# Seven products of quarters for the down projection of a gated MLP in fp32, in place of eight

## The chip, the cores and the metric

One core of a Trainium2 chip runs the whole program in one launch. The metric is device microseconds from the first to the last instruction of that core, as the median of several runs. TensorE (PE) multiplies, its weight loads are listed apart (PEld); VectorE (DVE), ScalarE (ACT) and GpSimd (POOL) do the elementwise work; SyncE (SP) issues most DMAs.

## The reference

Two sequences of 512 tokens, each with 16 meta tokens in front (T = 528), go through two layers: a mixer (attention in layer 0, a gated linear recurrence, hgrn, in layer 1) and then the MLP that the change is about. All in fp32:

```python
def conv_ffn(h, w_up, conv_w, conv_b, w_down):
    u = h @ w_up                                   # 1024 -> 5632
    u = sum(up[:, j:j + L] * conv_w[j] for j in range(3)) + conv_b
    val, gate = jnp.split(u, 2, axis=-1)           # 2 x 2816 gated features
    return (jax.nn.silu(gate) * val) @ w_down      # 2816 -> 1024

h = layer_norm(ALPHA * h + conv_ffn(h, ...), ln_gain[layer, 1], ln_bias[layer, 1])
```

The output is both sequences without the meta tokens.

## The kernel before

**Numbers in two parts.** TensorE multiplies in a rounded fp32 (F32R). Each operand x is split into a high part (a rounding copy, on ScalarE) and a low part (x minus the high part, on VectorE or GpSimd, `split` at L397 for features, `Weights.split` at L104 for weights), and each product is three matmuls: high by high, high by low, low by high. So every tile that TensorE reads costs one copy and one subtraction.

**Weights.** `Weights` (L78) walks a plan, one entry for each piece of up to 1024 columns, in the order of use. `get` takes a piece and keeps two ahead: `_load` issues its DMA into one of three raw buffers, `_split` makes the two parts into one of three pairs of buffers. For the down projection the low parts go to VectorE and GpSimd in turn (L154).

**The up stage** (from L1496) makes one of 22 pairs of feature blocks (j) at a time for both sequences. It computes the product of the first 1024 by two blocks with seven products of quarters in place of eight, with sums of weights made on GpSimd (`_mix`, L162), then the convolution, silu and the gate, and stores the gated block to `g_dr` in DRAM.

**The down stage** (from L1650) multiplies 2816 gated features (22 tiles of 128, index k) with the weights, one sequence after the other (s), the 8 output tiles of 128 in three groups (`MG`: 3, 3 and 2). In layer 0 a tile's 528 tokens go as two matmuls of 264 columns, in layer 1, where the meta tokens are dropped, as one of 512. In the first group of a sequence `load_g` (L1532) fetches each tile of features into one of four staging buffers and splits it, low parts on VectorE and GpSimd in turn; they stay for the other groups. When a group is done, VectorE reads PSUM, adds the residual in the same operation (L1670) and sums up for LayerNorm.

**LayerNorm** runs beside the matmuls as side work: a generator whose next step is emitted at a `tick()` between matmuls. Sequence 0's stands under sequence 1's matmuls, layer 0's sequence 1 under the start of the next layer. In layer 1 the last two output tiles of sequence 1 are done in two halves of 256 tokens (`last_group`, L1541), so that only the second half's LayerNorm is left behind the last matmul.

**Order.** The queue of each engine is fixed when the kernel is built: of the instructions that the planner takes to be ready, the one that stands first in the program goes first. On the chip each engine then runs its queue in that order, and waits on semaphores. PSUM has four tiles of two banks (`mtile`).

Of the kernel before, what the change touches and what calls it, by code (L numbers as in the profile page):

```python
# [19 lines left out]
D = 1024  # L20
META = 16
T = 528
# [36 lines left out]
MG = ((0, 1, 2), (3, 4, 5), (6, 7))  # L59
# [5 lines left out]
def down_pieces(ms):  # L65

    per = 1024 // (128 * len(ms))
    return [range(k, min(k + per, NJ)) for k in range(0, NJ, per)]
# [10 lines left out]
class Weights:  # L79


    def __init__(self, tc, pool, plan):
# [6 lines left out]
        self.kept = self.last = None  # L89
# [28 lines left out]
    def _load(self):  # L118
# [3 lines left out]
        for ap in () if place in self.loaded else aps:  # L122
# [13 lines left out]
    def _split(self):  # L136
# [13 lines left out]
        if key[0] == "mix":  # L150
            self.ready.append(self._mix(key, raws))
        else:
            n = math.prod(aps[0].shape) // 128
            on_dve = key[0] in ("rope", "v", "rows") or key[0] == "up" and (key[2] == 0 or key[3] in (0, 1, NJ + 2)) or key[0] == "down" and (self.ns % 2 or key[1:4] in ((1, 1, 2), (1, 1, 3)))  # L154
            self.ready.append(self.split(raws[0][:, :n], n, self.nc.vector if on_dve else self.nc.gpsimd))
# [24 lines left out]

    def get(self, key):
        assert self.plan[self.pos][0] == key, (self.plan[self.pos][0], key)
        last = len(self.plan)
        while self.ns < min(self.pos + 2, last):
            while self.nd < min(self.ns + 2, last):
                self._load()
            self._split()
        while self.nd < min(self.ns + 2, last):
# [65 lines left out]
def weight_plan(a):  # L254
# [15 lines left out]
    def block(layer):  # L270
        def down(s, g, i):
            n = 128 * len(MG[i])
            for ks in down_pieces(MG[i]):
                add(("down", layer, s, g, ks[0]), a[f"w_dn{layer}_{i}"][:, ks[0] * n : (ks[-1] + 1) * n])
# [13 lines left out]
        for s in range(2):  # L288
            for g in range(len(MG)):
                down(s, g, g)  # L290
        if layer == 1:
            down(1, 3, 2)
# [25 lines left out]
def tile_trunk(ctx: ExitStack, tc: tile.TileContext, a: dict, dbg=None):  # L318
# [16 lines left out]

    kr_dr = dram.tile([2, 2, 128, T], F32, tag="kr", name="kr_dr")
# [991 lines left out]
    def mlp_block(layer, dest):  # L1328
# [131 lines left out]
        def gated():  # L1460
            return [dp.tile([128, 2, T], F32, tag=f"c{half}", name="c", bufs=2 - half) for half in range(2)]
# [29 lines left out]
        for j in range(NPL, NJ):  # L1491
# [12 lines left out]
            nc.scalar.copy(e5, p5)  # L1504
            w = W.get(("mix", layer, j, 2))
# [15 lines left out]
            nc.sync.dma_start(g_dr[layer][j][:, :, f0:], ca)  # L1521
        close(d_cm, mix_cm[1], mix_cm[0], act_cm[1])

        g2_cm, g2 = open_pool(f"g2{layer}", side="right")
        g1_cm, g1 = open_pool(f"g1{layer}", side="right")
        e_cm, ep = open_pool(f"e{layer}", bufs=3, side="left")
        out = x_dr[2:4]
        t0 = META if dest == "out" else 0
# [231 lines left out]
```

## Time and profile before

| | us |
|---|---|
| median of 3 runs | 2959.49 (2959.28 to 2959.75) |
| the profiled execution | 2960.56 |
| its span, first to last instruction | 2958.7 |
| TensorE busy | 2841.1 |
| VectorE, ScalarE, GpSimd busy | 2014.8, 1339.4, 1314.3 |

The profile is of one execution. "Busy" is the time in which an engine had an instruction under way. Matmuls are pipelined: one of 264 columns is listed with 0.28 us, but the next begins after 0.12 us, so the pace is read from counts in a window. A row of a group gives line, engine, operation, output and inputs, shape and count; a wait gives the engine and line that waited, and what it waited for.

### The profile page before, as it was taken

To read this page: it belongs to the slowest core of one execution; us is meant where nothing else is said; L and a number is where in the kernel's file an instruction comes from. 1 tells how busy PE (TensorE), PEld (TensorE's weight loads), DVE (VectorE), ACT (ScalarE), POOL (GpSimd) and SP (SyncE) were. 2 spreads that over 40 slices of the span, in tenths; PEclk is the share of its full clock that TensorE was granted. 3 is DMA by queue.
4 is the path that set the end of the run, shared out by engine and by line. 5 is a ranking of instruction groups with operands and counts; after the bars stand their busy time and mean duration, and the time that the engine had idled before them with its cause. 6 is when DMAs were issued, how large, how long until landed. Compare 5 with 4: busy or idle time off the path is not lost.

```text
span 2958.7 us, 54755 instructions
## 1 busy us (share of the span) xinstructions
PE 2841.1 (96%) x22402; PEld 2749.5 (93%) x22402; DVE 2014.8 (68%) x2680; ACT 1339.4 (45%) x2275; POOL 1314.3 (44%) x889
## 2 busy tenths in 40 slices
PE   8889999999899999999999999999998999999997
PEld 8888999899899999999999999999998999998886
DVE  5687788866988888535275565555669888885346
ACT  3355555543634344434265554444436444444343
POOL 5344444453576776434242220000315767765333
PEclk9999999999999999999999999999999999999999
DMA  7423322357512222654477564444775222226543
GB/s 254 158 89 114 100 87 80 98 204 276 183 65 85 82 71 90 193 157 146 148 251 249 206 207 169 144 150 144 240 259 210 72 87 73 79 84 195 168 145 118
DMA packets 144138, 438.51 MB, mean 148 GB/s; under 512 B 19744, under 2 KB 28960, under 8 KB 125200
## 3 DMA queue, kind: packets, MB, share of 16 engines
q1 hardware_dynamic: 139392, 425.39, 43.1%
q10 hardware_dynamic: 3168, 5.43, 0.6%
q8 instruction: 176, 2.88, 0.4%
q0 software_dynamic: 1328, 4.19, 0.4%
q14 instruction: 74, 0.61, 0.1%
HBM read 288.22 MB, written 142.34 MB: 146 GB/s over the span
## 4 chain that ended last, share of the span: by engine, by line
PE 41%; DVE 3%; ACT 2%; DMA 2%; issue 1%; POOL 1%; DVEq 0%; ACTq 0%; POOLq 0%; SPq 0%
PE mm L414 5%; PE mm L416 5%; PE mm L415 5%; PE mm L1483 4%; PE mm L1484 4%; PE mm L1485 4%; PE mm L1660 2%; PE mm L1659 2%; PE mm L1658 2%; PE mm L892 1%; PE mm L893 1%; PE mm L891 1%; PE a L1065 1%; PE a L1038 1%; PE mm L422 1%
## 5 line engine op out<-in xcount | busy, mean ns | idle before, releaser
L414 PE MATMUL mm<-ah,w 128*128 128x264 f32 (+1 forms) x2528 | 735.8, 291 | 22.1 <-ACT w L106 9.5
L415 PE MATMUL mm<-al,w 128*128 128x264 f32 (+1 forms) x2528 | 722.3, 286 | 7.9 <-DVE al L402 7.9
L416 PE MATMUL mm<-ah,w 128*128 128x264 f32 (+1 forms) x2528 | 723.5, 286 | 4.5 <-DVE w L107 2.3
L414 PEld LDWEIGHTS mm<-ah,w 128*128 128x128 f32 x2528 | 481.1, 190 | 29.2 <-ACT w L106 9.5
L415 PEld LDWEIGHTS mm<-al,w 128*128 128x128 f32 x2528 | 481.9, 191 | 10.1 <-DVE al L402 9.5
L416 PEld LDWEIGHTS mm<-ah,w 128*128 128x128 f32 x2528 | 481.3, 190 | 4.9 <-DVE w L107 2.5
L107 POOL TENSOR_TENSOR w<-wraw,w 128x1024 fp32r<-128x1024 f32 (+3 forms) x126 | 267.3, 2124 | 431.8 <-ACT w L106 400.6
L106 ACT CAST w<-wraw 128x1024 fp32r<-128x1024 f32 (+3 forms) x262 | 242.6, 928 | 342.9 <-PE mm L1660 223.0
L1483 PE MATMUL mm<-ah,w 128*128 128x264 f32 (+1 forms) x1216 | 345.9, 284 | 7.3 <-ACT w L106 7.3
L1485 PE MATMUL mm<-ah,w 128*128 128x264 f32 (+1 forms) x1216 | 345.8, 284 | 2.5 <-DVE w L107 2.5
L1484 PE MATMUL mm<-al,w 128*128 128x264 f32 (+1 forms) x1216 | 344.9, 284 | 0.0
L1659 PE MATMUL mm<-gl,w 128*128 128x264 f32 (+1 forms) x1012 | 322.6, 319 | 4.2 <-DVE gl L402 4.2
L1660 PE MATMUL mm<-gh,w 128*128 128x264 f32 (+1 forms) x1012 | 321.2, 317 | 3.8 <-DVE w L107 2.0
L1658 PE MATMUL mm<-gh,w 128*128 128x264 f32 (+1 forms) x1012 | 323.1, 319 | 0.9 <-DVE acc L1670 0.9
L107 DVE TENSOR_TENSOR w<-wraw,w 128x1024 fp32r<-128x1024 f32 (+2 forms) x136 | 158.0, 1163 | 220.5 <-ACT w L106 220.4
L1483 PE MATMUL mm<-th,w 128*128 128x264 f32 (+1 forms) x912 | 260.5, 286 | 8.3 <-ACT e L1497 8.3
L1485 PE MATMUL mm<-th,w 128*128 128x264 f32 (+1 forms) x912 | 260.1, 285 | 0.0
L1484 PE MATMUL mm<-tl,w 128*128 128x264 f32 (+1 forms) x912 | 259.9, 285 | 0.0
L1483 PEld LDWEIGHTS mm<-ah,w 128*128 128x128 f32 x1216 | 230.3, 189 | 7.8 <-ACT w L106 7.8
L1485 PEld LDWEIGHTS mm<-ah,w 128*128 128x128 f32 x1216 | 230.2, 189 | 2.9 <-DVE w L107 2.9
L1484 PEld LDWEIGHTS mm<-al,w 128*128 128x128 f32 x1216 | 230.3, 189 | 0.0
L1660 PEld LDWEIGHTS mm<-gh,w 128*128 128x128 f32 x1012 | 191.2, 189 | 17.9 <-DVE w L107 2.2
(335 smaller groups left out, 7195.9 us busy)
## 6 DMA issues: line engine op xcount, KB each, us to landing
kept_dr<-w SPq DMA_DIRECT2D x73, 1024.0 KB, 6.6
w<-kept_dr SPq DMA_DIRECT2D x73, 1024.0 KB, 5.4
wraw<-w_up SPq DMA_DIRECT2D x88, 512.0 KB, 4.1
wraw<-w_dn SPq DMA_DIRECT2D x88, 384.0 KB, 3.3
wraw<-w_hg SPq DMA_DIRECT2D x32, 512.0 KB, 4.4
wraw<-w_dn SPq DMA_DIRECT2D x25, 512.0 KB, 3.6
gr<-g_dr SPq DMA_DIRECT2D x44, 264.0 KB, 3.4
gr<-g_dr SPq DMA_DIRECT2D x44, 256.0 KB, 3.6
```

The costliest lines, as they stand in the source:

```text
L106: self.nc.scalar.copy(h[:, :n], src)
L107: engine.tensor_tensor(l[:, :n], src, h[:, :n].bitcast(F32), op=ALU.subtract)
L414: mm(out, wh[:, ws], xh[:, x0 + k, cs], start=first and i == 0, stop=False)
L415: mm(out, wh[:, ws], xl[:, x0 + k, cs], start=False, stop=False)
L416: mm(out, wl[:, ws], xh[:, x0 + k, cs], start=False, stop=last and i == n - 1)
L422: mm(ps[c][:, :w], ones, src[:, t0 + c * w : t0 + (c + 1) * w], start=True, stop=True)
L1483: mm(out, wh[:, ws], bh, start=k == 0, stop=False)
L1484: mm(out, wh[:, ws], bl, start=False, stop=False)
L1485: mm(out, wl[:, ws], bh, start=False, stop=k == 3)
L1658: mm(o, wh[:, ws], gh[:, cs], start=k == 0, stop=False)
L1659: mm(o, wh[:, ws], gl[:, cs], start=False, stop=False)
L1660: mm(o, wl[:, ws], gh[:, cs], start=False, stop=k == NJ - 1)
```

## The change

The weight matrix (2816 by 1024) and the gated features (2816 by both sequences' tokens) are each cut into quarters: features into even and odd tiles (11 each) and, for each sequence, into the first and second half of its tokens; output tiles into 0 to 3 and 4 to 7. The four quarters of the result then come from seven products in place of eight, in the order 1, 6, 5, 7, 3, 2, 4. Products 1, 3 and 2 take a quarter of the features as it is, products 1, 2 and 4 a quarter of the weights; the other operands are sums of quarters:

- Sums of features for 6 and 5 are made in the up stage by two subtractions on GpSimd for each pair of tiles (`pair_sums`) and stored to a new array `t_dr`; for 7 and 4 one more subtraction on GpSimd is made at loading (`load_f`).
- Sums of weights for 6, 5, 7 and 3 are made at loading (`_down`), from up to three blocks; one sum stays in SBUF (`W.slots`).
- A product has two groups of two output tiles; each takes 11 tiles of features for both sequences, six matmuls for one output tile and both sequences (in layer 1 three matmuls of 512 columns, two sequences of 256 side by side). Product 4 is done for one sequence at a time.
- Each product's features are loaded and split again (`load_f`), for the next product in the second group of the running one, into 12 buffers for 11 tiles; low parts on VectorE, each third one on GpSimd.
- Results go from PSUM into the quarters that take them (an addition on VectorE, product 1 a copy on ScalarE); residuals are added in a step of their own.
- LayerNorm runs for halves of each sequence (264 or 256 tokens): the second halves are final after product 3, the first halves after product 4.

```diff
+NP = NJ // 2
+DOWN = "1657324"
+FBUFS = 12
...
+    def _down(self, key, raws):
+        q, g, b = key[2], *key[4:]
+        n = down_columns(b)                      # 1024, 1024, 768
+        even, odd = (nc.vector, nc.gpsimd) if b % 2 == 0 else (nc.gpsimd, nc.vector)
+        src = raws[0][:, :n]
+        if q not in "124":
+            s2 = self.slots[g, b]
+            if q == "6":
+                odd.tensor_tensor(src, src, raws[1][:, :n], op=ALU.add)
+                nc.vector.tensor_tensor(s2, src, s2, op=ALU.subtract)
+                src = s2
+            else:
+                odd.tensor_tensor(src, src, s2, op=ALU.add if q == "5" else ALU.subtract)
+        return self.split(src, n, even)
...
+        def pair_sums(i):
+            x, y = done.pop(2 * i), done.pop(2 * i + 1)
+            nc.gpsimd.tensor_tensor(x[:, :, hs[1]], x[:, :, hs[1]], x[:, :, hs[0]], op=ALU.subtract)
+            nc.gpsimd.tensor_tensor(x[:, :, hs[0]], y[:, :, hs[1]], x[:, :, hs[1]], op=ALU.subtract)
+            nc.sync.dma_start(t_dr[layer][i][:, :, t0:], x[:, :, t0:])
...
+        def load_f(q, i):
+            e = nc.gpsimd if i % 3 == 2 else nc.vector
...
+            if q in "165":
+                r = raw({"1": g(0, 0), "6": t[:, :, hs[0]], "5": t[:, :, hs[1]]}[q])
+            else:
+                r = raw(g(1, q in "73"))
+                if q in "74":
+                    less = raw(g(0, 1) if q == "7" else t[:, :, hs[0]])
+                    nc.gpsimd.tensor_tensor(r, r, less, op=ALU.subtract)
+            h = fp.tile([128, 2, wd], F32R, tag="fh", name="fh", bufs=FBUFS)
+            l = fp.tile([128, 2, wd], F32R, tag="fl", name="fl", bufs=FBUFS)
+            split(h, l, r, nc.scalar, e)
...
+        def group(q, s, g, after):
+            for i in range(NP):
+                if i % 4 == 0:
+                    wh, wl = W.get(("dn", layer, q, s, g, i // 4))
+                if (q, i) not in fs:
+                    load_f(q, i)
...
+                if after and g == 1:
+                    load_f(after, i)
+                tick()
...
+        def add_squares(q, xs, first=False):
+            for k, x in enumerate(xs):
+                sq = q if first and k == 0 else small("sq")
+                nc.scalar.activation(sq, x, AF.Square)
+                if sq is not q:
+                    nc.gpsimd.tensor_tensor(q, q, sq, op=ALU.add)
+
+        def shift_half(s, c):
+            x = [acc[m][:, s, hs[c]] for m in range(NK)]
+            nc.gpsimd.tensor_tensor(s1, x[0], x[1], op=ALU.add)
+            for k in (2, 3):
+                tt(s1, s1, x[k], op=ALU.add)
...
+            for k in range(4):
+                tt(x[k], x[k], mu, op=ALU.subtract)
+            for m in range(4, NK):
+                if c:
+                    tt(x[m], x[m], mu, op=ALU.subtract)
+                else:
+                    y = xs[m][:, s]
+                    nc.vector.scalar_tensor_tensor(y, y, ALPHA, mu, op0=ALU.mult, op1=ALU.subtract)
+                    nc.gpsimd.tensor_tensor(x[m], x[m], y, op=ALU.add)
+            add_squares(q, x[:4], True)
+            if c:
+                nc.gpsimd.tensor_tensor(s1, x[4], x[5], op=ALU.add)
+                for k in (6, 7):
+                    tt(s1, s1, x[k], op=ALU.add)
+                add_squares(q, x[4:])
+                yield from finish_half(s, c, [(0, s1), (1, q)])
...
+        def last_tiles(s, g, pss):               # product 4: two tiles, first half of sequence s
+            for y, ps in zip(x, pss):
+                tt(y, y, ps, op=ALU.add)
+            if g == 0:
+                nc.gpsimd.tensor_tensor(s1, *x, op=ALU.add)
+                add_squares(q, x)
+                return
+            if s == layer:                       # squares and tiles summed by TensorE instead
...
+            else:
+                for y in x:
+                    tt(s1, s1, y, op=ALU.add)
+                add_squares(q, x)
+            later(finish_half(s, 0, parts), 1)
+
+        def finish_half(s, c, parts):
...
+            for k in range(NK):
+                (nc.vector if k in (1, 4, 6) else nc.gpsimd).tensor_tensor(y, y, mu, op=ALU.subtract)
+            newton(r, v, t)
+            for k in range(NK):
+                nc.vector.scalar_tensor_tensor(y, y, prm[:, base + k : base + k + 1], r, op0=ALU.mult, op1=ALU.mult)
+                nc.scalar.activation(y, y, AF.Identity, bias=prm[:, base + 8 + k : base + 9 + k])
...
+                elif s == 0:
+                    split(act[0][0][:, k, h], act[0][1][:, k, h], y, nc.scalar, nc.gpsimd if k % 2 else nc.vector)
...
+        for n, q in enumerate(DOWN[:-1]):
+            for g in range(2):
+                pss = group(q, 0, g, DOWN[n + 1])
...
+            if q == "3":
+                for s in range(2):
+                    later(shift_half(s, 1))
...
+        for s in range(2):
+            later(shift_half(s, 0))
+        for s in range(2):
+            for g in range(2):
+                pss = group("4", s, g, None)
...
+                last_tiles(s, g, pss)
```

## Rows read from the trace of the kernel before

**Rows 1.** The page: the span, and busy time of each engine.

```profile
span 2958.7 us, 54755 instructions
PE 2841.1 (96%) x22402; PEld 2749.5 (93%) x22402; DVE 2014.8 (68%) x2680; ACT 1339.4 (45%) x2275; POOL 1314.3 (44%) x889
```

**Rows 2.** Busy time and count of each engine in six stretches of both layers.

```profile
core 0: us, PE busy (x) PEld busy (x) DVE busy (x) ACT busy (x) POOL busy (x), PEclk, DMA share, GB/s
820.00:1190.00 370.00, 365.93 (x2997) 365.72 (x2996) 314.84 (x273) 151.33 (x200) 260.65 (x127) 1.00 0.24 80
1202.50:1463.00 260.50, 253.78 (x2070) 252.45 (x2069) 103.08 (x115) 93.82 (x132) 102.83 (x59) 1.00 0.51 157
1240.00:1260.00 20.00, 20.00 (x167) 20.00 (x166) 4.92 (x6) 3.62 (x5) 4.97 (x3) 1.00 0.53 161
2682.50:2903.00 220.50, 217.59 (x936) 176.26 (x935) 86.49 (x94) 84.02 (x117) 88.66 (x51) 0.99 0.54 169
2700.00:2720.00 20.00, 20.00 (x87) 16.17 (x86) 7.99 (x8) 9.93 (x15) 14.07 (x9) 1.00 0.87 283
2903.00:2941.50 38.50, 34.96 (x273) 34.41 (x272) 32.43 (x39) 16.65 (x27) 12.34 (x10) 0.96 0.37 115
```

**Rows 3.** TensorE's waits, 1195 to 1475: us in total, times, longest.

```profile
PE mm L1660 <- DVE w L107: 2.0, 1, 2.0
PE mm L1659 <- DVE gl L402: 2.0, 1, 2.0
PE mm L1660 <- POOL w L107: 1.7, 1, 1.7
```

**Rows 4.** TensorE's longest wait from 2675 to the end.

```profile
PE mm L1623 <- DVE w L107: 3.5, 1, 3.5
```

**Rows 5.** Instructions by line or tile: ns min/median/max, first and last start, shapes.

```profile
L107 DVE TENSOR_TENSOR w<-wraw,w x136: 669/1218/2607, 9.5 to 2934.7; 128x1024 fp32r<-128x1024 f32 x80, 128x768 fp32r<-128x768 f32 x48, 128x512 fp32r<-128x512 f32 x8
L107 POOL TENSOR_TENSOR w<-wraw,w x126: 723/2362/3012, 25.2 to 2892.0; 128x1024 fp32r<-128x1024 f32 x63, 128x768 fp32r<-128x768 f32 x52, 128x256 fp32r<-128x256 f32 x8, 128x512 fp32r<-128x512 f32 x3
L402 POOL TENSOR_TENSOR gl<-gr,gh x44: 1285/1340/2243, 1199.4 to 2813.3; 128x528 fp32r<-128x528 f32 x22, 128x512 fp32r<-128x512 f32 x22
L402 DVE TENSOR_TENSOR gl<-gr,gh x44: 678/1095/2330, 1197.6 to 2811.9; 128x528 fp32r<-128x528 f32 x22, 128x512 fp32r<-128x512 f32 x22
L1511 DVE TENSOR_TENSOR u<-u,mm x38: 679/693/706, 832.0 to 2682.0; 128x528 f32<-128x528 f32 x19, 128x516 f32<-128x516 f32 x19
```

**Rows 6.** Timeline of VectorE and GpSimd: start us, duration us, what.

```profile
1199.42 3.54 POOL L402 TENSOR_TENSOR gl<-gr,gh 128x528 fp32r<-128x528 f32 x2
1211.25 1.81 POOL L107 TENSOR_TENSOR w<-wraw,w 128x768 fp32r<-128x768 f32 x1 [0.99 <-ACT w L106]
...
1199.95 1.83 DVE L402 TENSOR_TENSOR gl<-gr,gh 128x528 fp32r<-128x528 f32 x1
1201.71 0.69 DVE L1511 TENSOR_TENSOR u<-u,mm 128x528 f32<-128x528 f32 x1
1208.12 0.94 DVE L107 TENSOR_TENSOR w<-wraw,w 128x768 fp32r<-128x768 f32 x1
1211.29 2.33 DVE L402 TENSOR_TENSOR gl<-gr,gh 128x528 fp32r<-128x528 f32 x1
```

**Rows 7.** Groups by shape: busy us, mean ns, then idle before and releaser.

```profile
L107 POOL TENSOR_TENSOR w<-wraw,w 128x768 fp32r<-128x768 f32 x52 | 100.3, 1930 | 156.6 <-ACT w L106 125.4 <-DMA wraw<-w_dn 19.9 <-issue 11.1
L107 POOL TENSOR_TENSOR w<-wraw,w 128x256 fp32r<-128x256 f32 x8 | 5.8, 730 | 5.5 <-ACT w L106 5.5
L1001 DVE TENSOR_TENSOR qo<-qd,cross 128x256 f32<-128x256 f32 x32 | 13.4, 417 | 0.0
L1596 POOL TENSOR_TENSOR acc<-acc,gr 128x256 f32<-128x256 f32 x10 | 8.4, 873 | 15.0 <-ACT gr L1588 15.0
L1596 DVE TENSOR_TENSOR acc<-acc,gr 128x256 f32<-128x256 f32 x6 | 5.1, 873 | 0.0
```

More of the change, by code (lines that the diff above doesn't have):

```diff
@@ L121, in _load @@
         place = piece_place(key)
-        for ap in () if place in self.loaded else aps:
+        for i, ap in enumerate(() if place in self.loaded else aps):
+            if key[0] == "dn" and i == 2:
+                r = self.slots[key[4], key[5]]
+                self.nc.sync.dma_start(r, ap)
+                raws.append(r)
+                continue
             r = self.pool.tile([128, 1024], F32, tag="wraw", name="wraw", bufs=3)
@@ L270, in block, with down @@
     def block(layer):
[L271 to L274, printed above, removed]
+        def down(q, s):
+            blocks = {"1": "11", "6": "212211", "5": "11", "7": "22", "3": "12", "2": "12", "4": "22"}[q]
+            for g in range(2):
+                for b in range(3):
+                    cs = slice(1024 * b, 1024 * b + down_columns(b))
+                    aps = [a["w_dn"][layer, int(blocks[i]) - 1, int(blocks[i + 1]) - 1, g][:, cs] for i in range(0, len(blocks), 2)]
+                    add(("dn", layer, q, s, g, b), *aps)
         for s in range(2):
@@ L287, in block @@
                 add(("mix", layer, j, i))
[L288 to L292, printed above, removed]
+        for q in DOWN:
+            for s in range(2 if q == "4" else 1):
+                down(q, s)
     for ks in FIRST_ROWS:
@@ L1460, in gated, with load_pair @@
         def gated():
-            return [dp.tile([128, 2, T], F32, tag=f"c{half}", name="c", bufs=2 - half) for half in range(2)]
+            return [dp.tile([128, 2, T], F32, tag=f"c{half}", name="c", bufs=3 - 2 * half) for half in range(2)]
+        t0 = META if dest == "out" else 0
+        wd = half_of(t0)
+        hs = [slice(t0 + c * wd, t0 + (c + 1) * wd) for c in range(2)]
+        done = {}
+        def load_pair(i):
+            for j in (2 * i, 2 * i + 1):
+                if j not in done:
+                    done[j] = dp.tile([128, 2, T], F32, tag=f"p{j % 2}", name="p", bufs=1)
+                    nc.sync.dma_start(done[j][:, :, t0:], g_dr[layer][j][:, :, t0:])
+        def pair_sums(i):
[3 more added lines that the diff above has]
+            nc.sync.dma_start(t_dr[layer][i][:, :, t0:], x[:, :, t0:])
         first = gated()
@@ L1521, in mlp_block @@
             nc.sync.dma_start(g_dr[layer][j][:, :, f0:], ca)
+            if j > NPL:
+                done[j] = cs[0]
+        pair_sums(NP - 1)
         close(d_cm, mix_cm[1], mix_cm[0], act_cm[1])
[L1524 to L1528, printed above, removed]
[L1529 to L1539 removed]
```

280 lines of the change are left out of this document (135 added, 145 removed).

## The prediction

> **What bounds the kernel now.** The page first: TensorE is busy for 2841 of 2958.7 us, VectorE for 2015, GpSimd for 1314 [rows 1]. So columns taken from TensorE are worth their time only while the other engines can feed it, and that has to be read stage by stage. The windows come next [rows 2]: layer 0's down projection runs from 1202.5 to 1463 with TensorE busy 253.8 of 260.5 us, layer 1's from 2682.5 to 2941.5 in two stretches, 217.6 of 220.5 and 35.0 of 38.5. In all of them VectorE and GpSimd are busy for about 100 us each of 260: the stage has room. The up stage before it (820 to 1190) has little: VectorE 314.8 and GpSimd 260.7 of 370. Third, TensorE's waits: the few there are in the down stages end in a subtraction on VectorE or GpSimd, the low part of a gated feature (gl) or of a weight (w) [rows 3, 4]. TensorE waits there for nothing else of size. So the question is what the change asks of VectorE and GpSimd.
>
> **These two engines do not work side by side.** A low part of 528 or 512 columns takes VectorE 0.68 us at the least, 1.1 in the median and 2.33 at most; the same shape with one input in PSUM takes 0.68 to 0.71 always [rows 5]. The timeline shows why [rows 6]: at 1211.29 VectorE begins a low part 0.04 us after GpSimd began a weight of 1.81 us, and ends 0.56 us after it; at 1201.71 an addition from PSUM runs at its usual 0.69 us under a busy GpSimd. In the last rows of the kernel six subtractions on VectorE and ten on GpSimd of 256 columns, side by side, take 0.87 us each on both; alone they are 0.42 and 0.73 [rows 7]. Ten of 0.73 and six of 0.42 are 9.8 us of work, done in ten times 0.87 on the longer queue, 9.0 us with the gaps: 0.92. So I add up the times alone of all GpSimd work and of all VectorE work with two SBUF inputs, call it pair work, and take 0.92 us of wall for each us of it where both queues are full.
>
> The Trainium skill (SBUF — State Buffer, Who interferes with whom) says that a VectorE instruction with two SBUF inputs and a GpSimd instruction that reads SBUF exclude each other for a whole instruction. The rows agree but for 8%; by the page's rule alone the sum below would end 45 us later, at about 3065.
>
> **What is removed.** A matmul of 264 columns takes 20/167 = 0.1198 us, one of 512 columns 20/87 = 0.2299 [rows 2]. Layer 0 goes from 2112 to 1848 matmuls of 264 columns: 264 x 0.1198 = 31.6 us. Layer 1 goes from 924 to 792 of 512, with 264 of half width in both: 132 x 0.2299 = 30.3. Together 61.9 us, if TensorE is fed. It needs 221.4 us in layer 0 afterwards (253.0 before) and 182.1 + 31.6 = 213.7 in layer 1.
>
> **What is added, in pair work.** Prices alone, VectorE then GpSimd: 1024 columns 1.22 and 2.36 (medians), 768 columns 0.94 and 1.93, 528 columns 0.69 and 1.31, 256 or 264 columns 0.42 and 0.73 [rows 5 to 7].
> Weights: a group has two pieces of 1024 and one of 768, low parts on VectorE, GpSimd, VectorE: 4.5 us. There are 16 groups a layer, 72 us (before 44 pieces of 768 and 12 of 256 to 1024 columns, about 80).
> Sums of weights, new: 8.9 us in each of the two groups of product 6 (two operations a piece), 5.5 in those of 5, 7 and 3: 51 us.
> Gated features: 11 tiles a product, low parts of 8 on VectorE and 3 on GpSimd, 9.4 us; for 7 and 4 also 11 subtractions on GpSimd, 23.8. Seven products: 95 us, before 44 tiles, 22 x (0.69 + 1.31) = 44.
> Residuals in a step of their own, no longer with the read of PSUM: 12 x 0.69 = 8.
> LayerNorm by halves of 264 columns. Counted from the diff for layer 0, sequence 0: GpSimd 18 in the second half (1 + 3 + 1 + 4 sums, 5 subtractions, 4 splits), 8 in the shift of the first (1 + 4 + 3), 3 in the last tiles, 9 in its finish; VectorE 30 (2 + 4 + 4 + 2 + 1 + 3 + 2 + 8 + 4), 10, none, 18. Sequence 1 has no splits and its last finish comes behind the last matmul: 14 + 8 + 3 + 2 and 26 + 10 + 2. Together 65 x 0.73 + 96 x 0.42 = 88 us. In layer 1, with no splits at all, 57 and 88: 79. Before, sequence 0's stood under sequence 1's whole pass, and layer 0's sequence 1 under the next layer.
> The copies and squares go to ScalarE, busy 94 of 260 us [rows 2]: they stay hidden, and cost nothing unless their input is late.
>
> **Where it falls.** In products 1, 6, 5, 7 and 3 the pair work is 45 + 51 + 71 (features of 6, 5, 7, 3, 2 and 1) + 6 + 2 = 175 us, 161 of wall, against TensorE's 158 in layer 0 and 152 in layer 1. Buffers for 12 tiles let a product's features run one group ahead, so single products even out: +5 and +10. Now TensorE loses 7 us in layer 0's stage and 15 in layer 1's, most in what this replaces; I count no loss twice and set whole stages against each other.
> In products 2 and 4 it is 27 (weights) + 24 (features of 4) + 3 + 88 = 142, that is 130 us of wall against 63 on TensorE; in layer 1 133, 122 against 62. What comes late is what 4 multiplies with, since its features and weights stand in the same two queues behind the LayerNorm of the first halves; and what ends the stage is LayerNorm itself, which hgrn's first projection and the output wait for. So +67 and +60.
> Layer 0: 221.4 + 5 + 67 = 293 against 260.5, +33. Layer 1: 213.7 + 10 + 60 = 284 against 259, +25. The tail behind the last matmul is the same chain with one more small matmul: no change.
> Bounds. Below, sequence 1's 36 us in layer 0 (33 of wall) can be left until after hgrn has begun: +0 for layer 0. Above, both queues are never full all the time; 10% idle adds 13 us in each late part.
>
> **The up stage** gets 22 GpSimd subtractions a layer, 29 us, and 11 stores and four loads on SP's queue. TensorE loses 4 us of 370 there [rows 2]; some 6% more for the pair fits on average, but GpSimd also makes the weight sums there. I take +1 a layer; 0 if the gaps hold it, 27 if all of it is on the path. Behind each store on SP's queue stand weight loads; a late store delays them by the 2.6 us of its two subtractions, less than the two pieces that are ready ahead.
>
> **DMA.** 99 feature loads a layer in place of 44, 11 stores, about as many weight bytes: some 21 MB on 41 (157 GB/s x 260 us), 214 GB/s over 290 us, where 283 has been moved [rows 2]. Only product 6, three blocks of 512 KB for each 48 matmuls (5.75 us), asks 274 GB/s and more with the features beside it: up to 10 us a layer. I take none, as its pair work is as long, and keep 20 for the upper end.
>
> Sum: 33 + 25 + 2 = +60 on the profiled run's 2960.56. It stands 1.1 us over the median: 3020.
>
> **Rivals.**
> Queues free of each other: VectorE and GpSimd overlap well, or the order in the queues puts LayerNorm behind what TensorE needs. Then only GpSimd alone is too long in the late part: 65 x 0.73 + 14 x 1.31 + 6 x 2.36 = 80 us against 63, 74 against 62 in layer 1. Layer 0 221.4 + 5 + 17 = 243 (-17), layer 1 213.7 + 5 + 12 = 231 (-28): 2915. Wall is then 0.56 of pair work in the late part; the sign turns at 0.70, where the late parts take 99 and 93 us and the layers come to +2 and -4. For it: the rest of the stage had room. Against it: the collisions in [rows 6] and the paired subtractions in [rows 7].
> All hidden: TensorE's 61.9 us in full, 2899. Against it: GpSimd's 80 us alone.
> Sequence 1's LayerNorm in layer 0 waits, the early products lose nothing, and gain and loss nearly meet: within 0.2% only if layer 1's late part also shrinks by 25 us.
> Heavier than forecast: the up stage's 27 a layer or product 6's 10, or TensorE at its lower clock after the gaps (0.96 in the last stretch [rows 2], with a stall of 3.5 us [rows 4]): 3060 to 3085.
>
> **Chances.** Forecast 0.56, heavier 0.12, queues free 0.20, all hidden 0.06, a wash 0.06. A measurement of this kernel tells 0.2% (6 us) from no change. So faster 0.26, same 0.06, slower 0.68. The forecast's own range is 2985 to 3060; the range that takes in the free queues and the heavier case is 2912 to 3085.
>
> **What would show it.** In the profile after: TensorE near full in products 1 to 3 and about half busy in 2 and 4, its waits there on features and weights from GpSimd and VectorE, both with busy times that add up to far more than the wall; GpSimd's 264-column operations well over 0.73 us. Wrong it would be if TensorE stays over 95% to the end of product 4, or if the long waits are for DMA.

## The result, and the profile after

The kernel with seven products takes 3086.12 us (median of 4 runs, 3081.18 to 3087.44) against 2959.39 (2957.62 to 2959.75): 1.0428 times as long, 95% interval 1.0415 to 1.0441. It is slower, as forecast, but by 127 us where +60 was forecast: the time lies 26 us above the forecast's own range (2985 to 3060) and 1 us above the wide one (to 3085). The profiled execution took 3087.44 us, 126.9 more than the one before the change.

The page of the kernel after, span and busy time (answers to [rows 1]):

```profile
span 3085.6 us, 55124 instructions
PE 2847.3 (92%) x22028; PEld 2739.5 (89%) x22028; DVE 2262.9 (73%) x2916; ACT 1387.1 (45%) x2404; POOL 1543.2 (50%) x1082
```

374 matmuls fewer, and TensorE is busy for 6 us more. The windows of the kernel after show where (columns as in [rows 2], whose stages they answer to). The first seven are layer 0's products: 1, 6, 5, 7, 3, then 2 and 4. Then come layer 0's first five together; layer 1's first five, product 2, product 4; the tail; the up stage of layer 0:

```profile
1206.50:1250.10 43.60, 36.77 (x265) 36.11 (x265) 29.32 (x27) 21.08 (x30) 16.18 (x10) 0.88 0.80 258
1250.10:1283.90 33.80, 32.31 (x266) 32.10 (x265) 24.54 (x18) 10.37 (x16) 19.00 (x9) 1.00 0.74 236
1283.90:1327.60 43.70, 35.34 (x267) 34.49 (x266) 19.59 (x18) 11.16 (x15) 25.18 (x13) 0.92 0.55 173
1327.60:1374.70 47.10, 37.79 (x266) 36.31 (x265) 27.72 (x24) 14.22 (x21) 29.61 (x17) 0.86 0.63 194
1374.70:1410.90 36.20, 33.94 (x267) 33.73 (x266) 22.70 (x25) 15.41 (x22) 19.31 (x11) 0.95 0.73 231
1410.90:1472.00 61.10, 45.54 (x279) 43.44 (x278) 46.58 (x66) 24.96 (x55) 44.51 (x43) 0.78 0.45 140
1472.00:1538.00 66.00, 46.71 (x282) 42.47 (x281) 56.56 (x70) 32.16 (x65) 49.42 (x41) 0.77 0.51 156
...
1206.50:1410.90 204.40, 176.15 (x1322) 172.74 (x1322) 123.87 (x111) 72.24 (x102) 109.29 (x58) 0.92 0.68 217
...
2751.50:2943.70 192.20, 164.75 (x662) 128.89 (x662) 125.86 (x110) 69.14 (x99) 105.01 (x56) 0.94 0.70 220
2943.70:3005.10 61.40, 41.48 (x145) 32.00 (x144) 45.80 (x63) 25.11 (x52) 45.06 (x40) 0.78 0.49 151
3005.10:3070.00 64.90, 43.65 (x272) 39.91 (x271) 55.44 (x68) 26.68 (x53) 44.12 (x38) 0.79 0.44 137
...
3070.20:3085.60 15.40, 2.87 (x14) 2.20 (x13) 8.94 (x17) 6.20 (x15) 5.28 (x7) 0.72 0.20 68
820.00:1190.00 370.00, 365.47 (x2989) 365.05 (x2989) 326.89 (x272) 151.45 (x199) 284.95 (x149) 1.00 0.29 100
```

Read two things. Products 2 and 4, the "late" ones below, take 127 us in each layer, with TensorE granted 0.78 of its clock. That is what was forecast (130 and 122). The "early" ones, 1, 6, 5, 7 and 3, take 204.4 and 192.2 us where 163 and 162 were forecast. Layer 0's 204.4 split by the row: TensorE busy 176.2, which is 18 more than its 158 for these matmuls, and idle 28.2. In layer 1 it is busy for 13 more than 152, and idle for 27.5.

What TensorE waits for in layer 0's early products, 1206 to 1411 (columns as in [rows 3]):

```profile
PE mm L1654 <- POOL w L109: 17.6, 6, 5.8
PE mm L1653 <- DVE fl L436: 5.6, 2, 4.3
PE mm L1653 <- POOL fl L436: 2.8, 2, 2.5
PE mm L1652 <- ACT w L108: 1.6, 2, 1.1
```

Low parts again, but no longer of 2 us: three fifths of it are low parts of weights on GpSimd. One such wait, in product 5, by the timeline of the kernel after (start, duration, engine, what), and behind the "..." TensorE at the start of product 1:

```profile
1286.47 0.54 SPq L136 DMA_DIRECT2D wraw<-w_dn  x1
1289.99 1.04 ACT L108 CAST w<-wraw 128x1024 fp32r<-128x1024 f32 x1
1291.87 2.64 POOL L204 TENSOR_TENSOR wraw<-wraw,s 128x1024 f32<-128x1024 f32 x1 [0.41 <-DMA wraw<-w_dn]
1294.47 2.81 POOL L109 TENSOR_TENSOR w<-wraw,w 128x1024 fp32r<-128x1024 f32 x1
1293.19 1.89 DVE L436 TENSOR_TENSOR fl<-gr,fh 128x528 fp32r<-128x528 f32 x1 [0.89 <-ACT fh L433]
1297.34 0.59 PE L1654 MATMUL mm<-fh,w 128*128 128x264 f32 x1 [5.75 <-POOL w L109]
...
1211.32 0.59 PE L1653 MATMUL mm<-fl,w 128*128 128x264 f32 x1 [4.28 <-DVE fl L436]
1211.70 0.42 PE L1654 MATMUL mm<-fh,w 128*128 128x264 f32 x1
1211.92 0.42 PE L1652 MATMUL mm<-fh,w 128*128 128x264 f32 x1
...
1216.77 0.29 PE L1654 MATMUL mm<-fh,w 128*128 128x264 f32 x1
1216.89 0.28 PE L1652 MATMUL mm<-fh,w 128*128 128x264 f32 x1
```

The cast of the piece that TensorE waits for ends at 1291.03. Its low part would take GpSimd 2.36 us, but ahead of it in the queue stands the sum of another piece, which waits for a transfer issued at 1286.47 until 1291.87. Sum and low part then take 2.64 and 2.81 us with VectorE working beside them (its own low part, 0.70 alone, takes 1.89), and TensorE stands 5.75 us. The lower rows show the second price of a stall: after 4.28 us of idleness matmuls start 0.22 us apart (264 columns at 1.2 GHz), and only from 1216.77 on 0.12. Of layer 0's 1320 early matmuls 114 start at that slow pace, by the distances between their starts. At 0.1 us each these are some 11 of the 18 us of extra busy time (in layer 1, 49 matmuls and some 9 of 13 us); the rest is not taken apart.

### The profile page after: what moved, and what is told of

Same layout as the page of the kernel before. It is cut to its first block, busy times and chain, and to the rows that moved or that the text cites. A ratio compares the mean times of both kernels' runs of the same rounds, so it can differ in the third digit from the quotient of the medians.

```text
span 3085.6 us, 55124 instructions
## 1 busy us (share of the span) xinstructions
PE 2847.3 (92%) x22028; PEld 2739.5 (89%) x22028; DVE 2262.9 (73%) x2916; ACT 1387.1 (45%) x2404; POOL 1543.2 (50%) x1082
## 4 chain that ended last, share of the span: by engine, by line
PE 47%; DVE 12%; DMA 6%; POOL 5%; issue 4%; ACT 4%; SPq 0%; POOLq 0%; DVEq 0%; ACTq 0%
PE mm L1538 7%; PE mm L1536 7%; PE mm L1537 7%; PE mm L448 5%; PE mm L450 5%; PE mm L449 5%; DMA gr<-g_dr 2%; DMA wraw<-w_dn 2%; DVE fl L436 1%; DVE w L109 1%; DMA gr<-t_dr 1%; PE mm L926 1%; PE mm L927 1%; PE mm L925 1%; POOL gr L1610 1%
## 5 line engine op out<-in xcount | busy, mean ns | idle before, releaser
L449 PEld LDWEIGHTS mm<-al,w 128*128 128x128 f32 x2528 | 481.0, 190 | 8.7 <-DVE al L436 8.1
L109 POOL TENSOR_TENSOR w<-wraw,w 128x1024 fp32r<-128x1024 f32 (+1 forms) x101 | 232.2, 2302 | 261.6 <-ACT w L108 261.5
L1652 PE MATMUL mm<-fh,w 128*128 128x264 f32 (+2 forms) x968 | 325.9, 338 | 34.5 <-ACT fh L433 21.3
L1654 PE MATMUL mm<-fh,w 128*128 128x264 f32 (+2 forms) x968 | 325.7, 337 | 34.8 <-POOL w L109 31.1
L1653 PE MATMUL mm<-fl,w 128*128 128x264 f32 (+2 forms) x968 | 327.1, 338 | 26.0 <-DVE fl L436 17.9
L108 ACT CAST w<-wraw 128x1024 fp32r<-128x1024 f32 (+3 forms) x228 | 221.9, 976 | 160.5 <-PE mm L1654 48.2
L1654 PEld LDWEIGHTS mm<-fh,w 128*128 128x128 f32 x968 | 201.7, 208 | 52.5 <-POOL w L109 34.5
L1652 PEld LDWEIGHTS mm<-fh,w 128*128 128x128 f32 x968 | 200.7, 208 | 53.2 <-ACT fh L433 26.2
L1653 PEld LDWEIGHTS mm<-fl,w 128*128 128x128 f32 x968 | 200.9, 208 | 43.4 <-DVE fl L436 21.3
```

The source lines that it names most:

```text
L108: self.nc.scalar.copy(h[:, :n], src)
L109: engine.tensor_tensor(l[:, :n], src, h[:, :n].bitcast(F32), op=ALU.subtract)
L449: mm(out, wh[:, ws], xl[:, x0 + k, cs], start=False, stop=False)
L1652: mm(o, wh[:, ws], bh, start=i == 0, stop=False)
L1653: mm(o, wh[:, ws], bl, start=False, stop=False)
L1654: mm(o, wl[:, ws], bh, start=False, stop=i == NP - 1)
```

## The experiments

What had to be found was the cause in the early products. First theory: the lead, one weight piece of 5.75 us on TensorE against a chain of about that length. Rivals: the amount of work on the two engines; the bunching of a product's features in one half of the product before; one issuing queue for both chains; too few staging buffers.

A product's length is taken in the trace from its first matmul to the next product's first (product 4's to its last matmul). The kernel before took 2952 to 2961 us on the chips of these runs, so lengths are compared rather than whole times. They are of one run each; whole times are medians of 4 runs for the kernel after and e10, 10 for e19 and 12 each for e20 and e21, and single runs for the others. e4 and e7 leave the early products as they were and give 206.7 and 207.8, 192.0 and 191.4, so I read nothing into differences of some 4 us. In us:

```
kernel            whole    early L0, L1    late L0, L1
after             3086.1   204.4  192.2    127.1  126.5
e1_plain7         3057.9   188.2  181.6    127.1  125.4
e2_no_wsum        3019.9   175.4  165.0    126.5  122.8
e4_no_ln          2973.5   206.7  192.0     80.5   79.3
e5_one_load       2987.9   172.8  164.4    109.9  102.6
e6_ahead          3091.5   204.2  197.0    128.8  123.8
e7_ln_dve         3062.8   207.8  191.4    119.6  111.4
e8_floor          2867.6   169.3  158.9     64.0   61.5
e10_both          3067.2   203.0  196.6    118.1  113.2
e11_act_queue     3098.4   208.1  194.3    131.1  127.8
e12_staging       3076.4   195.9  184.2    130.8  124.9
e13_spread        3086.9   206.5  194.9    127.5  123.3
e14_spread_act    3103.5   207.2  201.3    134.0  125.3
e15_sum_act       3056.9   189.0  174.0    130.5  124.0
e16_early_dve     3001.5   175.8  163.1    119.4  110.6
e17_all_dve       2972.6   172.6  164.7    105.1  101.1
e19_dve_staging   2964.2   166.8  155.0    107.1   99.6
e20_mm_sums       2953.9   169.3  156.2    100.3   95.2
e21_wide          2956.4   170.4  155.6    101.4   93.1
```

**What is to blame: parts left out.** Product 7 with plain features; without sums of weights; without the LayerNorm's arithmetic; features loaded and split once; the last three together.

```diff
 e1: -                if q in "74":
     +                if q == "4":
 e2: -        if q not in "124":          # and products 6, 5 load their first block only
     +        if False:
 e5:          def load_f(q, i):
     +            if q != "1":
     +                fs[q, i] = fs["1", i]
     +                return
 e4: shift_half, finish_half, last_tiles keep the adding of products, the bias and the stores
 e8: e2, e4 and e5
```

> Product 7 multiplies with a plain quarter of the features, so 11 loads and 11 GpSimd subtractions a layer are left out of products 5 and 7, which took 43.6 + 47.2 us in layer 0 and 46.2 + 41.6 in layer 1. If the early products are slowed by the ring of load, subtraction, split and free buffer through four staging buffers: products 5 and 7 fall to about 70 us in each layer, 20 us less a layer, 3045. If pair work alone sets their pace: 14.4 us less of it, at most 13 us a layer and half of that since the pair was not full there (33 of 44 us), 3072. If it is the loads of weights and their sums: no more than 5 us a layer, 3076.

> All weight sums are left out: each piece is one raw load with its split, for products 6, 5, 7 and 3 too; 51 us of pair work and 12 loads a layer less. If pair work sets the pace of the early products, they fall from 204 and 192 us to near TensorE's own 158 and 152 plus the start's 12: 170 and 163, 60 us less in all, 3025. If it is the ring of feature loads through four staging buffers, products 5 and 7 keep most of their loss and only 6 and 3 gain: 190 and 180, 25 us less in all, 3060. The late part (127 and 126) keeps its time in both.

> LayerNorm's arithmetic behind the down projections is left out (sums, squares, means, subtractions, scaling, and the residual of the last four tiles of the first halves); the copies with the bias, the splits for hgrn and the stores stay. If its pair work is what makes products 2 and 4 long, they fall from 127 and 126 us to 63 to 72, TensorE's own time, and the tail of 16 us behind the last matmul to 5: about 2960. If features of 4 through the staging buffers are what is late, as in products 5 and 7: 90 to 100 us in each layer, about 3020.

> The features are loaded and split once, for product 1, and all later products multiply with these tiles: 88 loads, 66 splits and 22 subtractions a layer less, 86 us of pair work. If feature loads through the staging buffers slow the early products, those after product 1 run at TensorE's pace: 44 + 127 = 171 us in layer 0, 40 + 121 = 161 in layer 1, 64 us less. If the weights and their sums slow them: 6, 5, 7 and 3 keep 10 us each a layer, 25 us less in all. The late part loses 24 us of pair work in both cases: 105 in each layer, 43 us less. So 2980 or 3018.

> Gated features are loaded and split once, the sums of weights and their loads are left out, and the LayerNorm's arithmetic too: what is left beside TensorE is casts and low parts. Theory of the prediction: TensorE then runs at 0.12 us a matmul of 264 columns, early products 165 and 155 (158 and 152 and a start of a few us), late products 63 and 62, the kernel at about 2860 to 2870: the removed matmuls are worth their 62 us once nothing is late. Rival: a seventh of the matmuls is worth less, since TensorE runs part of the stage at its lower clock or waits for weights: early 175 and 165, late 80 and 79 as without LayerNorm, kernel 2910.

The LayerNorm is 47 us of each late part, and nothing of the early one. But 80.5 and 79.3 lie between e4's two theories (63 to 72, and 90 to 100): some 17 us of the late loss stay without it, in layer 0 all of them in product 4, which takes 48.7 us against product 2's 32.1. They fit the late features, whose repeated loads, splits and subtractions are worth 17 and 24 us there (e5). The early loss (35 and 33 us over e8's 169 and 159) falls to 4 to 6 us when either the sums of weights (e2) or the repeated features (e5) go: neither is too much alone. Product 7's second loads and subtractions (e1) are 16 and 11 us of it; the ring of buffers had expected 20, pair work at most 13. e8 bears out the worth of the removed matmuls: with nearly all else hidden TensorE needs 233 and 220 us from first to last product, 27 and 39 less than the stages of [rows 2]: 66, where the matmuls are 62. By the layer they are 32 and 30; e8 still loses 12 us in layer 0, most in product 1, and the kernel before lost 15 in layer 1.

**One more weight piece ahead (e6), loads from another queue (e11), more staging (e12), an even spread (e13, e14).**

```diff
 e6:  -        while self.ns < min(self.pos + 2, last):
      +        while self.ns < min(self.pos + (3 if self.deep() else 2), last):   # a fourth w; FBUFS = 11
 e11: -            self.nc.sync.dma_start(dst, ap)
      +            (self.nc.scalar if key[0] == "dn" else self.nc.sync).dma_start(dst, ap)
 e12: -                r = W.staging()[:, : 2 * wd].rearrange("p (s t) -> p s t", s=2)
      +                # four such, then four of: fp.tile([128, 2, wd], F32, tag="fr", bufs=4); FBUFS = 11
 e13: -            for g in range(2):
      -                for b in range(3):
      +            for b in range(3):
      +                for g in range(2):       # products 1, 6, 5, 7, 3; one load_f every second step
 e14: e13 and e11
```

> One more weight piece is made ahead of the one that TensorE uses (three in place of two, in a fourth pair of buffers; 11 feature buffers of each kind in place of 12). The pair work stays the same. Theory lead: the early products stall because a weight's chain (transfer, sum, cast, low part), about 5 us and its turns in the queues behind feature work, has one piece of 5.75 us as its lead. Then products 1, 6, 5, 7 and 3 go from 204 to about 175 us in layer 0 and from 192 to about 165 in layer 1, products 2 and 4 stay near 127 each, and the kernel comes to about 3030. Rival amount: the pair work by itself fills the early products. Then they stay at 200 or more and 190 or more, and the kernel within 10 us of the changed one.

> The loads of the down projection's weight pieces are issued from ScalarE's queue in place of SyncE's, where they stand among the feature loads that wait for staging buffers, and hold those up while they wait for a raw buffer. Theory queue (one issuing queue couples the two chains): early products 204 to 175 to 185 in layer 0, 192 to 165 to 175 in layer 1. Theory bunching (a product's 11 features are all made in the second group of the product before, with nothing of the kind in its first): 200 and 190 or more, since the order of the work stays. Kernel 3045 or 3085.

> Eight staging buffers for features in place of four (with 11 feature buffers of each kind in place of 12, to make room). Theory staging (a feature's load starts only when the fourth one before it has been split, so transfers of 3 to 4 us stand in the chain): early products 175 to 185 and 165 to 175. Theory queue: a smaller gain, to about 195 and 185, as SyncE waits less on slots. Theory bunching: 200 and 190 or more.

> In products 1, 6, 5, 7 and 3 the two groups go on side by side, block of weights by block, so each feature buffer is free after its block and the next product's features are made evenly over the whole product, one per two steps, in place of all in its second half. Same matmuls, same pair work, same buffers. Theory bunching: early products 170 to 180 in layer 0 and 160 to 168 in layer 1, products 2 and 4 as before at 127, kernel about 3030. Theories queue or staging: at most 10 us a layer from it, 195 and 184, as the same transfers wait for the same slots. Theory amount: no gain.

> Both: groups side by side, and the weight loads from ScalarE's queue. If bunching is all of it: as the spread alone. If the queue couples the chains beside it: 5 to 10 us a layer below it, at 169 and 159, the times that were measured with everything but casts and low parts left out.

My theory of the lead fell, and bunching with it; the theory of the queue stays open. TensorE's waits in layer 0's early products, of e6, then e13, then e12, and last two of ScalarE's there in e11:

```profile
PE mm L1662 <- DVE fl L444: 12.9, 8, 4.4
PE mm L1661 <- ACT fh L441: 9.4, 6, 2.9
PE mm L1663 <- POOL w L114: 5.2, 1, 5.2
```

```profile
PE mm L1691 <- DVE y L1819: 12.4, 3, 8.1
PE mm L1692 <- DVE fl L437: 6.3, 5, 3.8
PE mm L1693 <- POOL w L109: 3.4, 2, 3.2
```

```profile
PE mm L1659 <- POOL w L109: 20.4, 4, 6.9
PE mm L1658 <- DVE fl L436: 4.3, 1, 4.3
```

```profile
ACT w L108 <- POOL w L109: 24.8, 3, 12.5
ACT fh L433 <- POOL w L109: 12.9, 3, 7.7
```

With three pieces made ahead the waits for weights fall from 17.6 to 5.2 us, and features are late instead: product 7 goes from 47.2 to 53.6 us. e6 also has one feature buffer less, but ScalarE waits only 4.3 us for TensorE to free one (10.3 in the kernel after) and 34.6 us for GpSimd's subtractions that product 7 needs. With the spread the weights' waits fall too, and in layer 0, where the spread holds all four PSUM tiles, TensorE waits 12.4 us for PSUM to be read by a VectorE that is behind; layer 1, where it holds two and has no such wait, gains nothing either. Whatever gets its turn earlier, something else gets it later, and the sum of these runs stays at 204 to 208 in layer 0 and 194 to 201 in layer 1.

Only the eight staging buffers help, 8 us a layer: 195.9 and 184.2. That is what the theory of the queue had expected of them (195 and 185). e11 speaks against this theory, but it does not free the chains: it moves the weight loads into the queue of ScalarE, which makes the casts. By the last two rows ScalarE then stands for 38 us until GpSimd's low parts free a raw buffer; in the kernel after SyncE has such waits, 36.5 us, and ScalarE none. Neither a queue that makes nothing else nor a fourth raw buffer for weights was tried. So order and lead by themselves were not the limit.

**Amount, or length of the chain (e15); whose work it is (e16); the LayerNorm's part (e7, e10).**

```diff
 e15: -                odd.tensor_tensor(src, src, s2, op=ALU.add if q == "5" else ALU.subtract)
      +                nc.scalar.copy(src, s2)            # and so for product 6's two
 e16: -        even, odd = (nc.vector, nc.gpsimd) if b % 2 == 0 else (nc.gpsimd, nc.vector)
      +        even = odd = nc.vector
      -            e = nc.gpsimd if i % 3 == 2 else nc.vector
      +            e = nc.vector
      -                    nc.gpsimd.tensor_tensor(r, r, less, op=ALU.subtract)
      +                    tt(r, r, less, op=ALU.subtract)
 e7:  -                    nc.gpsimd.tensor_tensor(q, q, sq, op=ALU.add)
      +                    nc.vector.tensor_tensor(q, q, sq, op=ALU.add)    # and the other sums, subtractions
 e10: e6 and e7
```

> All of the LayerNorm's 65 additions and subtractions of GpSimd in the down stage go to VectorE but the low parts of what it multiplies with: some 50 operations a layer fall from 0.73 to 0.42 us, pair work 15 to 20 us less a layer. If the two engines exclude each other, products 2 and 4 go from 127 to 109 to 114 us in each layer, although VectorE, already the busier of the two, gets more work. If each queue counts by itself, VectorE's longer queue makes them slower than 127, or, where GpSimd's queue was the bound, they fall to 97 to 100. The early products stay at 204 and 192. Kernel 3050 to 3060 by exclusion.

> The two edits together, one weight piece more ahead and the LayerNorm on VectorE, with nothing left out: early products 175 and 165 by the theory of the lead, late ones 109 to 114, kernel about 2995 to 3010: still slower than before. By the rivals (amount of pair work early, queues by themselves late) 3080 or more.

> In place of each addition or subtraction that makes a sum of weights stands a copy of the same columns on ScalarE: the loads, the buffers and the number of steps from a weight's transfer to its low part stay, the sums (51 us a layer of VectorE's and GpSimd's time) go from the two engines. The sums themselves are left out of the computation. Theory amount: early products 175 to 180 in layer 0 and 165 to 170 in layer 1, as with sums and loads both left out. Theory chain: 195 or more and 185 or more, since the chain is as long as before. Products 2 and 4 stay at 127.

> The weights' sums and low parts, the features' low parts and the subtractions of products 7 and 4 all go to VectorE; GpSimd keeps the LayerNorm's share only. By the prices alone a GpSimd operation is 1.6 to 1.9 times as long, so the pair work of the early products falls from 175 to about 135 us, all of it in one queue. If the engines exclude each other, early products 172 to 182 and 162 to 172, and products 2 and 4 some 10 us shorter each layer. If they run beside each other, VectorE's queue gets longer than it was (124 us busy in 204) and TensorE waits more: 204 or more.

e10 misses both of its expectations. e15 is between its two theories: of the 29 and 27 us that e2 takes off, 15 and 18 come from the sums' work on the two engines alone; whether the rest is their loads or the steps of the chain (a ScalarE copy of 1.05 us stands where each sum was) stays open. e16 met its expectation (the late products are 8 and 16 us shorter, where some 10 were expected). Groups of one line by shape in layer 0's early products (busy, mean ns, then idle before), first of after:

```profile
L436 DVE TENSOR_TENSOR fl<-gr,fh 128x528 fp32r<-128x528 f32 x47 | 51.8, 1116 | 45.5 <-ACT fh L433 45.5
L436 POOL TENSOR_TENSOR fl<-gr,fh 128x528 fp32r<-128x528 f32 x18 | 28.0, 1554 | 29.1 <-ACT fh L433 29.1
L109 POOL TENSOR_TENSOR w<-wraw,w 128x1024 fp32r<-128x1024 f32 x9 | 22.8, 2530 | 7.9 <-ACT w L108 7.9
L109 DVE TENSOR_TENSOR w<-wraw,w 128x1024 fp32r<-128x1024 f32 x8 | 12.0, 1500 | 0.5 <-ACT w L108 0.5
```

and of e16:

```profile
L436 DVE TENSOR_TENSOR fl<-gr,fh 128x528 fp32r<-128x528 f32 x66 | 46.8, 728 | 7.6 <-ACT fh L433 7.4
L109 DVE TENSOR_TENSOR w<-wraw,w 128x1024 fp32r<-128x1024 f32 x16 | 19.5, 1219 | 3.8 <-ACT w L108 3.8
```

With GpSimd silent VectorE does 66 low parts of features in 46.8 us; beside it, 47 took 51.8. Its windows, early and late, layer 0 then 1:

```profile
1201.10:1376.90 175.80, 165.24 (x1321) 162.74 (x1321) 137.37 (x167) 73.10 (x102) 3.31 (x2) 0.99 0.80 253
1376.90:1496.30 119.40, 86.11 (x557) 80.42 (x556) 101.82 (x154) 57.20 (x118) 64.22 (x63) 0.84 0.50 156
2710.30:2873.40 163.10, 153.28 (x661) 123.18 (x661) 134.08 (x165) 71.19 (x101) 2.99 (x2) 1.00 0.84 266
2873.40:2984.00 110.60, 82.25 (x417) 70.87 (x416) 96.09 (x149) 50.51 (x102) 55.86 (x56) 0.83 0.51 154
```

VectorE's busy time grows only from 123.9 to 137.4 while GpSimd's 109.3 all but go, and 29 us go from each layer's early products. In the late ones e7 shows the same: the LayerNorm's work moved to the busier of the two engines makes them 8 and 15 us shorter (109 to 114 was expected; layer 0's 119.6 misses that). e10 is e7's gain and e6's nought: 1.037 times the kernel before (1.0342 to 1.0397).

**A version.** All of it on VectorE (e17); with eight staging buffers (e19); the LayerNorm's sums over tiles as products with ones on TensorE (e20); subtractions of a mean from four tiles at a time (e21).

```diff
 e17: e16 and e7;   e19: e17 and e12
 e20: -            nc.vector.tensor_tensor(s1, x[0], x[1], op=ALU.add)
      -            for k in (2, 3):
      -                tt(s1, s1, x[k], op=ALU.add)
      -            mm(ps, ones, s1, start=True, stop=True)
      +            for k in range(4):
      +                mm(ps, ones, x[k], start=k == 0, stop=k == 3)
 e21: -            for k in range(NK):
      -                y = acc[k][:, s, h]
      -                tt(y, y, mu, op=ALU.subtract)
      +            for k in range(0, NK, 4):
      +                y = acs[:, k : k + 4, s, h]
      +                tt(y, y, over(mu, 4), op=ALU.subtract)
```

> As the last one, and the LayerNorm's additions and subtractions on VectorE too. By exclusion: early products as there, products 2 and 4 at 105 to 112 in each layer (127 before, 119 and 111 with the LayerNorm alone moved), kernel 2985 to 3010, still slower than before the change. By two free queues: over 3086.

> The last one with eight staging buffers for features: 0 to 8 us a layer less, as eight staging buffers by themselves took 8 us off each layer's early products. Kernel 2975 to 3010: not faster than before the change by any theory here, since TensorE needs 62 us less but the LayerNorm's 47 us a layer stay behind products 2 and 4.

> The version with all of the work on VectorE and eight staging buffers, and the LayerNorm's sums over tiles (22 additions of 264 columns and 6 of squares a layer) made by TensorE's products with ones, which run for 0.39 us each and find room there. VectorE loses 28 x 0.42 to 0.5 = 12 to 14 us a layer of its 100 and 91. If VectorE's amount bounds products 2 and 4: 107 goes to 94 to 98 and 100 to 88 to 92, kernel 2938 to 2948, 0.5% faster than before the change. If the chain does: 105 and 98 or more, kernel 2955 to 2965.

> The same, and the subtractions of a mean from four tiles in one instruction of 1056 columns in place of four of 264 (0.42 each; 528 columns take 0.70, so about 0.15 us of each instruction doesn't depend on its columns). 42 instructions a layer fewer, 6 us. If VectorE's amount is the bound: 3 to 6 us a layer less than the last, kernel 2926 to 2940. If the chain is: no gain, or some loss, since what follows the subtraction starts after all four.

e17 came out under its range for the kernel, and e19 too: at 2964.2 us it is 1.0018 times the kernel before (1.0005 to 1.0031). Its early products, 166.8 and 155.0 us, run at the pace of e8's, with TensorE busy for 162 and 152 us, and the layers' gain is all spent in the late ones. e20 is just faster than before the change, by 0.16%: 2953.86 against 2958.32 us, 0.9984 (0.9974 to 0.9993), a third of what was expected, and e21 is at 0.9990 (0.9981 to 0.9999). e20's windows, early and late, layer 0 then 1:

```profile
1201.20:1370.50 169.30, 162.42 (x1321) 160.94 (x1321) 134.25 (x165) 72.37 (x101) 1.65 (x1) 1.00 0.84 267
1370.50:1470.80 100.30, 86.58 (x596) 81.10 (x595) 92.00 (x191) 56.95 (x119) 7.51 (x9) 0.93 0.57 175
2685.30:2841.50 156.20, 153.03 (x661) 125.90 (x661) 132.17 (x165) 71.65 (x101) 1.61 (x1) 0.98 0.88 282
2841.50:2936.80 95.30, 81.51 (x463) 72.42 (x462) 84.48 (x182) 49.63 (x101) 0.00 (x0) 0.91 0.56 172
```

Against e19 VectorE lost 8 and 7 us of late work, and the late parts 7 and 4. It is still busy for 92 of 100 and 84 of 95 us there, so its amount may still bound them; that is not shown. In e21 it lost more (2239 against 2246 us busy over the kernel), and the time did not fall. The chain of dependent steps, the other theory, may be why; no run shows it.

## Why the prediction was wrong, step by step

**The step that failed** is "Buffers for 12 tiles let a product's features run one group ahead, so single products even out: +5 and +10". Measured it was +46 and +40 over TensorE's 158 and 152. TensorE was not near full there, the sign that the prediction had named: busy for 176 of 204 us, as against 92 of 127 in the late products.

The pair work itself came out near its forecast of 161 us of wall: by the starts and lengths of the records, at least one of the two engines had some of it under way for 168 us in layer 0 and for 162 in layer 1. What failed was to let it and TensorE's 158 meet in the mean. In layer 0 TensorE was idle for 28 us and the pair for 36; GpSimd by itself waited 45 us for transfers (weights 30, features 15). Two chains share the two in-order queues, each waits behind the other's instructions, as in the timeline above, and one weight piece and one buffer over a product's tiles are all their lead. At a load of about 1 (161/158) TensorE waited 28 us in layer 0, and was busy for 18 more, some 11 of them by the lower clock. At a load of 135/158, in e16, it was busy 165 and waited 10.6.

Load alone does not set it: e15 leaves the two engines the same pair work as e2, and its early products are 14 and 9 us longer. Which of both, exclusion or GpSimd's long instructions inside the chain, brings more of e16's gain isn't told apart: that run takes away both.

**The late products** were right in kind and size, +67 and +60 forecast, about +64 measured on 63 and 62 (127.1 and 126.5). GpSimd and VectorE were busy there for 94 and 103 of 127 us, and by the records at least one of them for all but 3 (in layer 1 for all but 8): here the pair was full, or nearly. The LayerNorm's share is 47 us (e4). That late features and weights stood behind it is in e4 too: with it gone, product 2 runs in 32.1 us in place of 61.1. But product 4 still takes 48.7, as product 7 took 47.1, and of the pair work that the prediction counted only 54 us are left there, 50 of wall against 63 on TensorE: it would have put e4 at 63, not at 80.5. The step that failed in the early products fails there too.

**Pair work.** The two engines do hinder each other: 1116 against 728 ns for a feature's low part. The Trainium skill (SBUF — State Buffer, Who interferes with whom) has them exclude each other for whole instructions. By that rule the prediction's sum came to about 3065, nearer to the 3086 measured. But what the forecast lacks is not in the late products, where 127 us are 0.90 and 0.95 of the 142 and 133 of pair work. It is in the early ones, where the pair was not full, so the rate was not the error.

**Removed matmuls**, 61.9 us: borne out by e8, whose products after the first take 32.0 and 29.9 us each in the early parts where 31.6 and 30.3 were worked out. **Tail**, no change: 15.4 us against 17.2. **Up stage**, +1 a layer: layer 0's down stage starts 4 us later (1206.5 against 1202.5), and from layer 0's last product to layer 1's first it is 6 us less (1213.5 against 1219.5). The runs above have the same first up stage, and their down stages start at 1200.1 to 1209.3, so the 4 us tell nothing; GpSimd's 24 us more in 370 were hidden. **DMA**, none: layer 0's stage moved 63 MB (190 GB/s over 331.5 us) where 62 were worked out, and no wait of TensorE's of size names a transfer. The rate was no limit: the early products had 217 GB/s here, and in e20 they ran at 267 and 282. But a weight that lands 5.4 us after its issue is part of the chain, and more staging was worth 8 us a layer. Product 6, for which I kept 10 us, was layer 0's shortest at 33.8; in layer 1 it took 34.4 against 30.

**Rivals.** The heavier one (0.12) came nearest: 3060 to 3085. But of its three reasons only the lower clock after gaps counted, some 11 and 9 us in the early products, and the 28 us a layer of waits are not in it: that its number came so near is luck. Queues free of each other is refuted by the time itself (2915 forecast), and by e16 and e7, where moving work to the busier engine makes the kernel faster.

## What to carry to other kernels

Where two chains feed TensorE from the same in-order queues, do not set mean loads against each other. With the feeding engines at about TensorE's time (161 against 158 us) this kernel lost 46 us, in waits and again in the clock after the longer ones, and more lead or another order only changed who was late; at 135 against 158 it lost 18. Before you take columns from TensorE, count what the change adds to VectorE and GpSimd in the same stretch, and try GpSimd's share on VectorE alone: here that took 29 us off each layer's early products. Work at the end of a stage (here the LayerNorm of all rows behind the last product) was on the path whatever the products saved: set it against the product time that is left to cover it.

## What the runs showed of the hardware

After a stall of 4.28 us TensorE's matmuls of 264 columns start 0.22 us apart from 1211.32 to 1216.77, and 0.12 apart after that, with no wait between. The granted clock was 0.92 in layer 0's early products, in which TensorE was idle for 14% of the time. It was 0.99 in e16's, which had 10.6 us of waits.

A VectorE low part of 528 columns took 728 ns in the mean with GpSimd all but silent, and 1116 beside it. Moving a stage's elementwise work from GpSimd to VectorE, its busier neighbour, made that stage shorter. One VectorE instruction of 1056 columns with a repeated input took 1.25 us (e21), where a row of four of 264 took 1.46 (e20).
